# The probability blocks of neighbourhood attention go through DRAM, head by head, with the scores spaced evenly and six output tiles kept

## The chip, the cores and the metric

The kernel runs on one NeuronCore of one Trainium2 chip. The metric is device time in microseconds: 1574.57 us, the median of three runs before the change (1574.06 to 1577.02). The engines are named as in the profile: PE is TensorE (PEld its weight loads), DVE VectorE, ACT ScalarE, POOL GpSimd, SP the sync engine, which here only issues DMAs.

## The reference

The reference is one step of a trunk of two layers over 512 latent tokens (8 rows of 64) and 128 prompt tokens, 1024 wide. Layer 0 mixes by neighbourhood attention, layer 1 by grouped-query attention; a gated ConvFFN follows each. The change lies in layer 0's attention, of which this matters:

```
s_lat = einsum('brqhd,brkwhd->bhrqkw', qg, kg) * scale        # 8 x 16 window of keys, 16 heads of 64
s_lat = where(col_ok, s_lat + rpb[:, dr, dc], -inf)           # learned relative position bias
s_ctx = einsum('brqhd,bchd->bhrqc', qg, k_ctx) * scale        # 128 context keys
p     = softmax(concatenate([s_lat, s_ctx], -1), -1)
o     = einsum(p_lat, vg) + einsum(p_ctx, v_ctx)
op    = blocked_attention(qp, kp, vp)                         # the 128 prompt tokens
x     = x + gate * rmsnorm(o @ w_o)
```

## The kernel before, in words

All matrices are float32. A projection is split into a high and a low part of each operand (hi by a cast on ACT, lo by a subtraction on DVE or POOL), and three matmuls (hi·hi, hi·lo, lo·hi) stand for one. The weights come through four buffers `wr`, and their halves through four `wh` and four `wl`.

Layer 0's attention lasts from about 55 to 350 us. Three streams of work are interleaved in the order in which they are written, and each engine runs its part in order:

- `stream()` yields the projections in pieces. Each pair of heads has eight pieces of Q (`qk`, 256 columns for four, 384 for four) and eight of K; each group of four heads has fifteen pieces of V (`vp`). A piece is six to nine matmuls. `fill()` runs one piece. When the pieces are used up, the early part of the output projection (`y`, `m0.part0`) takes their place, three matmuls of 512 columns per piece.
- `ada0`, one step of which is eight small matmuls (`ada`) on two weight tiles of 512 KB, whose buffers are loaded again behind them.
- the heads. `Head.scores(slot)` handles one of four query blocks: two matmuls into `s` (L119), the bias and the running minimum on DVE (L980), the exponential on ACT (L984), the reciprocal on DVE (L988), the scaling on POOL (L989) and a transposition within 32 x 32 blocks on DVE (L992). The result stays in `p`.

A 32 x 32 transposition leaves each block in its own partitions. What is still wanted is an exchange of four partition groups of 32 with four blocks: block k of group q goes to block q of group k. The method `exchange` (L999) does this for a pair of heads by sixteen DMAs from `p` to `px`, both in SBUF, on SP's queue. `p` holds a pair and has two buffers, `px` holds a pair and has one.

`values` (L1004 on) multiplies V with `px` for a pair (24 matmuls into `po`) and ACT copies the result to the pair's output tile `of` (L1021). There are two such tiles; the first six pairs are written to DRAM (`of0d`, L486) and read back as `ofr` (L1032) when `o_split` makes the high and low part (`oh`, L1035, and `ol`, L1036) for the output projection. Every four heads the prompt's attention runs in three parts: `p0` scores (`sp`), `p1` transposes (`tp`), `p2` values (`po<-ptp`).

The order of the pieces in step h, in which head h + 1 is scored, is written in strings: `f` is a piece, `s0` to `s3` the scores, `x` the exchange, `v` the values, `a` a step of ada, `p0` to `p2` the prompt. `ORDER[0]` holds for even steps, `ORDER[1]` for odd ones, `ORDER0` for step 0 and `ORDER2` from step 13 on. A scheduler keeps PE in the written order and may move other engines' instructions a little past each other.

Of the kernel before, what the change touches and what calls it, by code (L numbers as in the profile page):

```python
# [40 lines left out]
NPX = 1  # L41
NOF = 2
# [9 lines left out]
ORDER0 = "s0 f s1 f f s2 f f s3 f f x f f a f f f f f".split()  # L52
ORDER = (
    "s0 f s1 f f s2 f f s3 f f x f f a f f f f f".split(),
    "p0 f f s0 f f p1 s1 f f s2 f f s3 f v a p2 f".split(),
)
ORDER2 = (
    ("s0 s1 f s2 f s3 f f x" + 16 * " f").split(),
    "p0 s0 f s1 f f p1 s2 f s3 f v p2 f".split(),
# [15 lines left out]
def raw_ap(ap, offset, dims):  # L75
    return bass.AP(tensor=ap.tensor, offset=ap.offset + offset, ap=[list(d) for d in dims])
# [30 lines left out]
def hybrid_step(ctx: ExitStack, tc: tile.TileContext, A, O):  # L107
# [19 lines left out]
    def f32(t):  # L127
        return t.bitcast(F32)
# [346 lines left out]
    of0, of0d = {}, {}  # L475
# [6 lines left out]

    def of_store(p):

        of0d[p] = dr.tile([P, T], F32, name=f"of0d{p}")
        nc.sync.dma_start(of0d[p], of0.pop(p))  # L486
# [300 lines left out]
    with l_na:  # L787
# [161 lines left out]
        pair, px = [None], [None]  # L949

        class Head:
# [42 lines left out]
            def exchange(self):  # L994

                px[:] = [ap.tile([P, 4, 2, 4, 3, QD], F32, tag="px", name="px", bufs=NPX)]
                for q in range(4):
                    for k in range(4):
                        nc.sync.dma_start(px[0][QD * k : QD * k + QD, q], self.pair[QD * q : QD * q + QD, k])  # L999

            def block(self, s0, s1):

                c0 = 12 * QD * self.b + 3 * QD * s0[0] + QD * s0[1]
                d = 3 * QD * (s1[0] - s0[0]) + QD * (s1[1] - s0[1])  # L1004
                return raw_ap(px[0], c0, [px[0].ap[0], [d, 2], [24 * QD, 4], [1, QD]])
# [22 lines left out]
        def o_split(p):  # L1028
            hi, lo = osp0[p]
            if p in of0d:  # L1030
                x = wp.tile([P, T], F32, tag="wr", name="ofr")
                nc.sync.dma_start(x, of0d[p])  # L1032
            else:
                x = of0[p]
            nc.scalar.copy(hi, x)  # L1035
            nc.vector.tensor_sub(lo, x, f32(hi))  # L1036
# [50 lines left out]
        for h in range(H):  # L1087
            nxt = Head(h + 1) if h + 1 < H else None
# [3 lines left out]
            for i, step in enumerate(order):  # L1092
                if step == "f":
                    if i < len(order) - 1 or h % 4 or not h:
                        fill()
                elif step == "a":
                    next(ada0, None)
                elif step[0] == "s" and nxt:
# [23 lines left out]
            if h % 2 and h < 12:  # L1122
                of_store(h // 2)
            before = head
# [859 lines left out]
```

## Time and profile before

| what | value |
|---|---|
| median of three runs | 1574.57 us |
| the profiled execution | 1577.02 us, its span 1575.0 us |
| granted clock of TensorE, mean of the span | 0.993 |
| PE, DVE, ACT, POOL busy, share of the span | 96%, 66%, 54%, 45% |
| HBM read and written | 216.34 and 28.31 MB, 155 GB/s over the span |
| exchanges of the sixteen heads | 128 DMAs of 96 KB |
| outputs stored and read back | 6 and 6 DMAs of 320 KB |

The profile page gives busy times and the groups of instructions; views of the trace give the waits of an engine by what released them, the instructions in order of time, and the busy time and granted clock of any stretch. A matmul's weights are loaded beside the previous matmul, so PE and PEld overlap. The duration of a matmul is modelled and overlaps the next; from start to start is the true spacing. A wait is put down to the semaphore that came last by the profile.

### The profile page before, as it was taken

Reading aid. Unit: us, or ns where it says so; the run is one execution under the profiler, and the core shown is the slowest. Engines: PE = TensorE matmul, PEld = TensorE weight load, DVE = VectorE, ACT = ScalarE, POOL = GpSimd, SP = SyncE. Lnnn points to the kernel's source line nnn. Section 1 sums busy time; section 2 is a strip of 40 time slices with the busy share of each in tenths; the row PEclk is TensorE's granted clock in tenths of the full one; section 3 lists DMA queues with packets and bytes.
Section 4 is the critical chain, followed back from the end, with each engine's and each line's share of the span. In section 5 each row is a group of like instructions: output and inputs, shape, how many; then the busy total and the mean of one; then the engine's idle time right before and its main releaser. Section 6 shows DMA issues by size and latency. Waiting matters only on the chain.

```text
span 1575.0 us, 25917 instructions
## 1 busy us (share of the span) xinstructions
PE 1507.6 (96%) x9549; PEld 1335.4 (85%) x9549; DVE 1037.2 (66%) x1680; ACT 843.3 (54%) x1608; POOL 710.2 (45%) x606
## 2 busy tenths in 40 slices
PE   6989999789999999999999999999999999999998
PEld 5978788568899999988887887877899999988886
DVE  4554444538887666776465878772988887886554
ACT  4554645535555555654544447773656665554443
POOL 1445535313445555534443555541325566553433
PEclk9999999999999999999999999999999999999999
DMA  9556767557366656368575331004633334448664
GB/s 325 140 154 178 203 154 213 150 163 249 105 206 198 218 194 194 104 222 289 178 244 184 101 108 55 2 1 166 203 110 114 106 110 151 132 155 267 215 220 136
DMA packets 204538, 260.50 MB, mean 165 GB/s; under 512 B 13724, under 2 KB 155260, under 8 KB 204412
## 3 DMA queue, kind: packets, MB, share of 16 engines
q1 hardware_dynamic: 194576, 252.27, 50.8%
q10 hardware_dynamic: 9836, 6.59, 2.2%
q8 instruction: 75, 1.23, 0.3%
q14 instruction: 51, 0.42, 0.1%
HBM read 216.34 MB, written 28.31 MB: 155 GB/s over the span
## 4 chain that ended last, share of the span: by engine, by line
PE 63%; DVE 5%; ACT 2%; issue 2%; POOL 1%; DMA 1%; ACTq 0%; POOLq 0%; DVEq 0%; SPq 0%
PE acc L119 18%; PE ux L119 17%; PE uz L119 8%; PE gp L119 5%; PE uy L119 4%; PE po L119 2%; PE y L119 2%; PE s L119 2%; PE tp L122 2%; PE ada L119 1%; DMA wr<-in_ffn_w_up 1%; DVE t L1303 1%; ACT gp L1714 1%; ACT t L1301 0%; DVE wl L182 0%
## 5 line engine op out<-in xcount | busy, mean ns | idle before, releaser
L182 POOL TENSOR_TENSOR wl<-wr,wh 128x1024 fp32r<-128x1024 f32 x70 | 172.8, 2474 | 240.8 <-ACT wh L180 231.1
L1226 POOL TENSOR_TENSOR wl<-wr,wh 128x1024 fp32r<-128x1024 f32 x76 | 183.6, 2439 | 42.2 <-ACT wh L1225 38.3
L119 PE MATMUL ux<-B,wh 128*128 128x322 f32 x832 | 201.0, 313 | 1.4 <-ACT u L1280 1.1
L1303 DVE SCALAR_TENSOR_TENSOR t<-C,cw,t 128x644 f32<-128x644 f32 x176 | 156.2, 888 | 55.5 <-ACT t L1301 54.9
L119 PE MATMUL acc<-wh,alo 128*128 128x512 f32 x440 | 172.3, 392 | 0.4 <-DVE alo L1195 0.3
L119 PE MATMUL acc<-wl,ahi 128*128 128x512 f32 x440 | 172.0, 391 | 0.0
L119 PE MATMUL acc<-wh,ahi 128*128 128x512 f32 x440 | 171.9, 391 | 0.0
L180 ACT CAST wh<-wr 128x1024 fp32r<-128x1024 f32 x140 | 145.6, 1049 | 43.3 <-DMA wr<-in_ffn_w_down 33.1
L119 PE MATMUL uz<-B,wh 128*128 128x322 f32 x640 | 156.2, 312 | 1.5 <-ACT v L1280 1.5
L119 PEld LDWEIGHTS ux<-B,wh 128*128 128x128 f32 x832 | 144.2, 189 | 4.4 <-ACT u L1280 2.2
L1195 DVE TENSOR_TENSOR alo<-ain,ahi 128x384 fp32r<-128x384 f32 (+1 forms) x88 | 82.7, 957 | 88.3 <-ACT ahi L1193 87.8
L119 PE MATMUL ux<-B,wl 128*128 128x322 f32 x416 | 129.9, 312 | 4.2 <-DVE wl L1226 4.2
L119 PE MATMUL qk<-hT,wh 128*128 128x384 f32 (+1 forms) x512 | 124.1, 315 | 1.7 <-DVE qs L892 1.7
L1226 POOL TENSOR_TENSOR vl<-wr,vh 128x1024 fp32r<-128x1024 f32 x38 | 106.2, 2794 | 26.2 <-ACT vh L1225 25.9
L119 PEld LDWEIGHTS uz<-B,wh 128*128 128x128 f32 x640 | 110.9, 189 | 4.9 <-ACT v L1280 2.0
L1225 ACT CAST wh<-wr 128x1024 fp32r<-128x1024 f32 x84 | 85.0, 1049 | 45.8 <-DVE wr L1249 45.3
L1301 ACT ACTIVATE t<-C,cw 128x644 f32<-128x644 f32 x88 | 78.6, 893 | 51.0 <-DVE C L1331 39.2
L182 DVE TENSOR_TENSOR wl<-wr,wh 128x1024 fp32r<-128x1024 f32 x70 | 91.7, 1320 | 17.3 <-ACT wh L180 16.7
L119 PE MATMUL uz<-B,wl 128*128 128x322 f32 x320 | 99.6, 311 | 0.4 <-POOL wl L1226 0.3
L119 PEld LDWEIGHTS acc<-wh,alo 128*128 128x128 f32 x440 | 82.6, 188 | 18.9 <-DVE alo L1195 1.2
L119 PEld LDWEIGHTS acc<-wl,ahi 128*128 128x128 f32 x440 | 82.6, 188 | 18.0 <-POOL wl L182 0.3
L119 PEld LDWEIGHTS acc<-wh,ahi 128*128 128x128 f32 x440 | 82.6, 188 | 17.8
(258 smaller groups left out, 3831.6 us busy)
## 6 DMA issues: line engine op xcount, KB each, us to landing
wr<-in_ffn_w_up SPq DMA_DIRECT2D x88, 512.0 KB
wr<-in_ffn_w_down SPq DMA_DIRECT2D x88, 512.0 KB
wr<-in_ada_w SPq DMA_DIRECT2D x72, 512.0 KB
act<-act SPq DMA_DIRECT2D x44, 321.0 KB
wr<-in_na_w_qkv SPq DMA_DIRECT2D x24, 512.0 KB
px<-p SPq DMA_DIRECT2D x128, 96.0 KB
mod<-modrow SPq DMA_DIRECT2D x20, 512.0 KB
ain<-act SPq DMA_DIRECT2D x44, 192.0 KB
```

The costliest lines, as they stand in the source:

```text
L119: pe(nc.tensor.matmul(*a, **k))
L122: pe(nc.tensor.transpose(*a, **k))
L180: i = nc.scalar.copy(hi, raw)
L182: j = (low or nc.vector).tensor_sub(lo, raw, f32(hi))
L1195: pin(nc.vector.tensor_sub(lo[:, 0 : c1 - c0], ain[:, 0 : c1 - c0], f32(hi[:, 0 : c1 - c0])))
L1225: nc.scalar.copy(hl[0], src)
L1226: low.tensor_sub(hl[1], src, f32(hl[0]))
L1301: nc.scalar.activation(t, taps(0), AF.Identity, bias=cw[:, 3, n : n + 1], scale=cw[:, 1, n : n + 1])
L1303: nc.vector.scalar_tensor_tensor(t, taps(d), cw[:, w, n : n + 1], t, op0=ALU.mult, op1=ALU.add)
L1714: nc.scalar.activation(self.pt[i].rearrange("p (a b) -> p a b", a=2), sv, AF.Exp, bias=nm, scale=-1.0, accum_out=su)
```

## The change

`exchange` is replaced by two methods. `write` stores a head's `p` to a DRAM tile `pd` in one DMA (128 rows of 6144 bytes, 768 KB). `read` loads it back into `px` in four DMAs, each of 32 partitions with four runs of 1536 bytes (192 KB). `p` now holds one head and still has two buffers; `px` holds a pair and has one. A head is written in the step that scores it (`w`; head 0 by `W` in step 0), read in the next step (`x`; the last head by `y`), and the values of a pair come in the even step after that. The four scores of a head are spread over a step, and the prompt's parts lie later in it. `of` has six buffers, and the store and reload of outputs are gone, so `o_split` reads `of` itself. The split of pair 6 follows the values in step 14, and the values of the last pair come after all early pieces of the output projection.

```diff
-NPX = 1
-NOF = 2
+NOF = 6
...
-    "s0 f s1 f f s2 f f s3 f f x f f a f f f f f".split(),
-    "p0 f f s0 f f p1 s1 f f s2 f f s3 f v a p2 f".split(),
+    "f s0 f s1 f v f s2 f x f a f f s3 f f f f w f".split(),
+    "s0 f f p0 f s1 f x f s2 p1 f a s3 f f p2 f f w".split(),
...
-    def of_store(p):
-
-        of0d[p] = dr.tile([P, T], F32, name=f"of0d{p}")
-        nc.sync.dma_start(of0d[p], of0.pop(p))
...
-                if not self.b:
-                    pair[:] = [ap.tile([P, 4, 2, 4, 3, QD], F32, tag="p", name="p", bufs=NPT)]
-                self.pair = pair[0]
-                self.p4 = self.pair[:, :, self.b]
+                self.p4 = ap.tile([P, 4, 4, 3, QD], F32, tag="p", name="p", bufs=NPT)
...
-            def exchange(self):
-
-                px[:] = [ap.tile([P, 4, 2, 4, 3, QD], F32, tag="px", name="px", bufs=NPX)]
-                for q in range(4):
-                    for k in range(4):
-                        nc.sync.dma_start(px[0][QD * k : QD * k + QD, q], self.pair[QD * q : QD * q + QD, k])
+            def write(self):
+
+                self.pd = dr.tile([P, 4, 12 * QD], F32, name=f"pd{self.h}")
+                nc.sync.dma_start(self.pd, self.p4.rearrange("p k n m i -> p k (n m i)"))
+
+            def read(self):
+
+                if not self.b:
+                    px[:] = [ap.tile([P, 4, 2, 12 * QD], F32, tag="px", name="px", bufs=1)]
+                self.px = px[0]
+                src = self.pd.rearrange("(q i) k c -> i q k c", q=4)
+                for k in range(4):
+                    nc.sync.dma_start(self.px[QD * k : QD * k + QD, :, self.b], src[:, :, k])
...
-            if p in of0d:
-                x = wp.tile([P, T], F32, tag="wr", name="ofr")
-                nc.sync.dma_start(x, of0d[p])
-            else:
-                x = of0[p]
-            nc.scalar.copy(hi, x)
-            nc.vector.tensor_sub(lo, x, f32(hi))
+            nc.scalar.copy(hi, of0[p])
+            nc.vector.tensor_sub(lo, of0[p], f32(hi))
...
-            nxt = Head(h + 1) if h + 1 < H else None
+            if h == H - 1:
+                break
+            nxt = Head(h + 1)
...
-                elif step == "x" and nxt:
-                    nxt.exchange()
-                elif step == "v":
-                    values((before, head))
+                elif step == "W":
+                    head.write()
+                elif step == "w":
+                    nxt.write()
+                elif step == "x":
+                    head.read()
+                elif step == "y":
+                    nxt.read()
+                elif step == "v" and h:
+                    values(done)
+                    if h == 14:
+                        o_split(6)
...
-            if h % 2 and h < 12:
-                of_store(h // 2)
-            before = head
+            if h % 2 == 0:
+                done = head, nxt
...
-            if h == 13:
-                o_split(6)
-            if h == 14:
-                drain(work)
-                for t in range(NT):
-                    m0.part0(t, 6)
+        drain(work)
+        for t in range(NT):
+            m0.part0(t, 6)
+        values(done)
         o_split(7)
```

SP's queue at the first heads, before. `px<-p` is an exchange, `wr<-in_na_w_qkv` a weight load of a projection (8x128 for Q or K, 4x256 for V), `wr<-in_ada_w` one of ada, `of0d` the store of an output:

```order
L176 DMA wr<-in_na_w_qkv 128x8x128
L999 DMA px<-p 32x768 x16
L295 DMA wr<-in_ada_w 128x1024 x2
L176 DMA wr<-in_na_w_qkv 128x4x256 x2
L295 DMA wr<-in_ada_w 128x1024 x2
L486 DMA of0d_1330<-of_1300 128x640
L176 DMA wr<-in_na_w_qkv 128x8x128 x4
L999 DMA px<-p 32x768 x16
L295 DMA wr<-in_ada_w 128x1024 x4
```

The same place with the change, from the V loads ahead of the first write to the loads behind head 2's write (`pd_970`, `pd_1114` and `pd_1311` are the DRAM tiles of heads 0 to 2):

```order
L175 DMA wr<-in_na_w_qkv 128x4x256 x2
L988 DMA pd_970<-p 128x1536
L997 DMA px<-pd_970 32x4x384
L294 DMA wr<-in_ada_w 128x1024 x2
L997 DMA px<-pd_970 32x4x384 x3
L988 DMA pd_1114<-p 128x1536
L175 DMA wr<-in_na_w_qkv 128x8x128
L294 DMA wr<-in_ada_w 128x1024
L997 DMA px<-pd_1114 32x4x384 x4
L294 DMA wr<-in_ada_w 128x1024
L988 DMA pd_1311<-p 128x1536
L175 DMA wr<-in_na_w_qkv 128x8x128 x2
```

The V weights of the second group stand before the first write instead of behind the first exchange. The Q load behind head 1's write is that of heads 6 and 7, the two behind head 2's write are K of these heads and Q of heads 8 and 9, which PE reaches in steps 3 and 4. Next in this queue come head 2's reads, two ada loads, head 3's write, two more ada loads and then head 3's reads.

PE at the start of step 1, before. `tk` transposes the new keys of the prompt for the output, `sp` is the prompt's scores, and `kh`, `kl` are the high and low part of the keys:

```order
L122 MATMUL tk<-ident,kp 128x128
L119 MATMUL sp<-kh_745,qs_673 128x128
L119 MATMUL sp<-kl_611,qs_673 128x128
L119 MATMUL sp<-kh_983,qs_829 128x128
L119 MATMUL sp<-kl_613,qs_829 128x128
L119 MATMUL sp<-kh_746,qs_674 128x128
L119 MATMUL sp<-kl_612,qs_674 128x128
```

The same place with the change:

```order
L121 MATMUL tk<-ident,kp 128x128
L118 MATMUL s<-kh_978,qs_829 128x384
L118 MATMUL s<-kl_613,qs_829 128x384
L118 MATMUL qk<-hT_114,wh 128x384
L118 MATMUL qk<-hT_114,wl 128x384
L118 MATMUL qk<-hT_115,wh 128x384
```

The first score of head 2, which needs the pair's new keys, now stands directly behind `tk`, and the prompt's scores follow after twelve matmuls of the projection.

SP's queue at the end of the stage, before:

```order
L1032 DMA ofr<-of0d_2926 128x640
L1032 DMA ofr<-of0d_3300 128x640
L176 DMA wr<-in_na_w_o 128x2x512 x4
L999 DMA px<-p 32x768 x16
L354 DMA mod<-modrow_2_83 128x1024
```

And with the change, from the write of head 14 on:

```order
L988 DMA pd_3591<-p 128x1536
L175 DMA wr<-in_na_w_o 128x2x512 x2
L997 DMA px<-pd_3591 32x4x384 x4
L988 DMA pd_3691<-p 128x1536
L175 DMA wr<-in_na_w_o 128x2x512 x2
L997 DMA px<-pd_3691 32x4x384 x4
L353 DMA mod<-modrow_2_83 128x1024
```

The last exchange has become head 15's write and its four reads, with two loads of output weights between them.

More of the change, by code (lines that the diff above doesn't have):

```diff
@@ L51 @@
 CTX = 2
-ORDER0 = "s0 f s1 f f s2 f f s3 f f x f f a f f f f f".split()
+ORDER0 = "s0 f f s1 f f W f f s2 f a f s3 f x f f f f f w".split()
 ORDER = (
-    "s0 f s1 f f s2 f f s3 f f x f f a f f f f f".split(),
-    "p0 f f s0 f f p1 s1 f f s2 f f s3 f v a p2 f".split(),
+    "f s0 f f s1 f v f s2 f x f a f f s3 f f f f w f".split(),
+    "s0 f f p0 f s1 f x f s2 p1 f a s3 f f p2 f f w".split(),
 )
 ORDER2 = (
-    ("s0 s1 f s2 f s3 f f x" + 16 * " f").split(),
-    "p0 s0 f s1 f f p1 s2 f s3 f v p2 f".split(),
+    "f s0 f s1 f v s2 f s3 f x f f f f f w f f f f f f y".split() + 12 * ["f"],
+    "s0 f x f s1 p0 f s2 f p1 s3 f p2 f f f f w".split(),
 )
@@ L474, in hybrid_step @@
     opool = r_na.enter_context(pool("o0", 1, "right"))
-    of0, of0d = {}, {}
+    of0 = {}
     def of_tile(p):
@@ L947, in na_table @@
             return tb
-        pair, px = [None], [None]
+        px = []
         class Head:
@@ L1004, in block @@
                 d = 3 * QD * (s1[0] - s0[0]) + QD * (s1[1] - s0[1])
-                return raw_ap(px[0], c0, [px[0].ap[0], [d, 2], [24 * QD, 4], [1, QD]])
+                return raw_ap(self.px, c0, [self.px.ap[0], [d, 2], [24 * QD, 4], [1, QD]])
         def values(two):
@@ L1097, in hybrid_step @@
                     next(ada0, None)
-                elif step[0] == "s" and nxt:
+                elif step[0] == "s":
                     nxt.scores(int(step[1]))
-                elif step == "x" and nxt:
-                    nxt.exchange()
-                elif step == "v":
-                    values((before, head))
+                elif step == "W":
[10 more added lines that the diff above has]
+                        o_split(6)
                 if pr and step == "p0":
```

## The prediction

> **What bounds the kernel now.** I read the page first, then who PE waits for in the stretch that the change touches, then the granted clock by ten microseconds, then the DMA queue of SP.
>
> ```profile
> span 1575.0 us, 25917 instructions
> PE 1507.6 (96%) x9549; PEld 1335.4 (85%) x9549; DVE 1037.2 (66%) x1680; ACT 843.3 (54%) x1608; POOL 710.2 (45%) x606
> DMA packets 204538, 260.50 MB, mean 165 GB/s; under 512 B 13724, under 2 KB 155260, under 8 KB 204412
> ```
>
> PE sets the end: it is busy for 96% of the span, and no other engine is above 66% (its weight loads overlap it). The change adds and removes no matmul, so it can move the time only through what PE loses between matmuls. It touches the neighbourhood attention, about 55 to 350 us. There PE waits for this (columns: who waits for whom, us in total, times, longest):
>
> ```profile
> PE vp L119 <- POOL wl L182: 6.9, 6, 2.5
> PE y L119 <- ACT oh L1035: 5.7, 2, 3.9
> PE po L119 <- DMA tr<-in_k_rpb: 3.7, 1, 3.7
> PE tk L122 <- ACT kp L906: 3.3, 1, 3.3
> PE vp L119 <- DVE kl L864: 3.2, 2, 1.6
> PE sp L119 <- ACT kh L863: 2.2, 5, 0.6
> PE tp L122 <- POOL pp L708: 1.8, 1, 1.8
> PE sp L119 <- DVE kl L864: 1.8, 7, 0.3
> PE qk L119 <- DVE qs L892: 1.7, 1, 1.7
> PE po L119 <- ACT qs L891: 1.6, 1, 1.6
> PE po L119 <- DMA px<-p: 1.2, 1, 1.2
> PE tk L122 <- DVE p L992: 1.0, 1, 1.0
> PE ada L119 <- DMA wr<-in_ada_w: 0.5, 1, 0.5
> ```
>
> These rows add up to 34.6 us. The second loss is the clock (columns by stretch: length, busy PE, PEld, DVE, ACT, POOL, granted clock, DMA share, GB/s):
>
> ```profile
> 90.00:100.00 10.00, 7.92 (x38) 7.36 (x39) 5.00 (x13) 6.00 (x20) 3.09 (x4) 0.83 0.56 122
> 110.00:120.00 10.00, 6.42 (x41) 5.78 (x38) 2.01 (x7) 5.30 (x14) 6.10 (x4) 0.94 0.94 273
> 120.00:130.00 10.00, 10.00 (x82) 9.28 (x82) 3.92 (x12) 5.52 (x12) 7.72 (x7) 0.89 0.80 177
> 240.00:250.00 10.00, 10.00 (x83) 7.89 (x82) 5.44 (x17) 6.43 (x20) 4.14 (x6) 1.00 1.00 298
> 280.00:290.00 10.00, 7.48 (x51) 5.12 (x52) 1.12 (x3) 1.14 (x4) 0.07 (x1) 0.83 0.64 183
> 310.00:320.00 10.00, 4.49 (x18) 2.93 (x20) 5.98 (x17) 4.52 (x13) 3.33 (x5) 0.84 0.67 192
> 320.00:330.00 10.00, 10.00 (x56) 7.34 (x53) 3.76 (x13) 4.25 (x13) 1.17 (x2) 0.82 0.44 156
> 90.00:350.00 260.00, 227.00 (x1587) 196.75 (x1588) 117.06 (x328) 129.59 (x357) 111.32 (x117) 0.97 0.67 181
> ```
>
> Each stretch below 1.00 follows waits, and loses ten times its missing share: 1.7 + 0.6 + 1.1 + 1.7 + 1.6 + 1.8 = 8.5 us. So 34.6 + 8.5 = 43.1 us is all that the change can work on. Most of it has nothing to do with the exchange itself; the queue that carries the exchange explains why:
>
> ```profile
> SPq L999 <- DVE p L992: 67.7, 8, 30.0
> 90.75 12.83 SPq L999 DMA_DIRECT2D px<-p  x16
> 104.79 0.94 SPq L176 DMA_DIRECT2D wr<-in_na_w_qkv  x2
> ```
>
> SP works in order. Its eight exchanges stand at the head of its queue for 67.7 us until the last probabilities are transposed, then hold it for about 12.8 us each, and what is traced behind them leaves late. The two V weight loads leave at 104.79, and their splits come too late for the V product: that is the wait of 2.5 us in the first row of PE's waits. The exchange costs PE more through what is queued behind it than through its own landing.
>
> **The change part by part.**
>
> *The SP queue.* In the new order the V weights stand ahead of the first write, and the Q and K loads follow writes whole heads before their use (the order of SP shows it). Behind a waiting write are then loads needed a head later, some 18 us (295 us for 16 heads), not the next ones. Of the 6.9 us for wl I leave 1.0, and with them goes the low clock of 110 to 130 us (0.6 + 1.1). Gain 5.9 + 1.7 = 7.6. SP itself issues 5 DMAs per head in place of 16 per pair, and no stores and reloads of outputs; it is off PE's path, so that is worth nothing by itself.
>
> *The exchange, longer and earlier.* It becomes a write of 768 KB and four reads of 192 KB per head. No row shows such a round trip. These are the nearest:
>
> ```profile
> px<-p SPq DMA_DIRECT2D x128, 96.0 KB
> of0d<-of SPq DMA_DIRECT2D x6, 320.0 KB
> 313.63 1.02 SPq L1032 DMA_DIRECT2D ofr<-of0d  x2
> 316.79 0.73 ACT L1035 CAST oh<-ofr 128x640 fp32r<-128x640 f32 x1 [1.20 <-DMA ofr<-of0d]
> 280.15 1.02 SPq L295 DMA_DIRECT2D wr<-in_ada_w  x2
> 281.99 4.50 PE L119 MATMUL po<-px,vt 128*64 128x256 f32 x24 [3.67 <-DMA tr<-in_k_rpb]
> ```
>
> A reload of 320 KB from DRAM is in use 3.2 us after its issue. The last part of an exchange, whose issue ended when the ada loads began at 280.15, was in use 1.8 us later (the row blames a table load, but it is the exchange that PE had been waiting for). With 1.8 us of latency and 298 GB/s, the rate of the stretch at full DMA share, 768 KB take 1.8 + 2.6 = 4.4 us, once written and once read.
>
> Cover in the new order: head 3's reads stand in SP behind the ada loads of its own step, which wait for PE's ada product. From there to the values PE has three scores, 24 matmuls of 384 columns and 24 of 256:
>
> ```profile
> 78.40 0.33 PE L119 MATMUL qk<-hT,wh 128*128 128x384 f32 x1
> 78.57 0.34 PE L119 MATMUL qk<-hT,wl 128*128 128x384 f32 x1
> 343.17 0.39 PE L119 MATMUL y<-wh,oh 128*128 128x512 f32 x1
> 343.40 0.39 PE L119 MATMUL y<-wl,oh 128*128 128x512 f32 x1
> 327.93 0.34 PE L119 MATMUL s<-kl,qs 128*128 128x384 f32 x1
> 331.11 1.14 DVE L992 STREAM_TRANSPOSE p<-p 128x384 f32<-128x384 f32 x2 [0.63 <-POOL p L989]
> ```
>
> One start follows the next after 0.17 us at 384 columns and 0.23 at 512, so about 0.12 at 256, by the columns. The cover is 6 x 0.17 + 24 x 0.17 + 24 x 0.12 = 8.0 us. The two ada loads of 512 KB and the reads make 1.8 MB, 6.2 + 1.8 = 8.0 us. It is even; I take 1.0 us of wait there and at heads 7 and 11, which have two loads ahead as well, and none at heads 1, 5, 9 and 13, which have at most one. The bounds are nothing, if a load is hidden, and 3.5 us each, if both come on top. For the last pair, head 15's scores to the values has 54 matmuls of 512 columns, 12.4 us. Against them: 4.3 us from the last score to its transpose (327.93 to 332.25), 4.4 to write, 4.4 to read: 13.1. Two output weight loads stand between write and reads, 3.5 us of traffic if none of it is hidden, so the wait lies between 0.7 and 4.2; I take 2.0. All: 3 x 1.0 + 2.0 = 5.0 us in place of 3.7 + 1.2 + 1.6 + 0.5 = 7.0; the clock term at 280 us I leave, for it can follow the last pair's wait. Gain 2.0.
>
> *The ring of six.* Twelve DMAs of 320 KB go. The output splits at the end of head 13's scores no longer wait for reloads: the 3.9 us of the longer oh wait becomes about 1.0, what one cast (0.73 us) and its subtraction take before the first product; the 1.9 us at the very end stays, since that chain is unchanged. One of the two clock stretches after 310 us goes, 1.7. Gain 2.9 + 1.7 = 4.6.
>
> *The scores, evenly spaced.* DVE, ACT and POOL do the same work in other places, so I price only the queueing: qs 1.7 to 0.5, kl before vp 3.2 to 1.6. The prompt scores move back by a score and two pieces of projection, but the first score of the next head now stands right behind tk and needs the same keys, so of tk, kh and kl (3.3 + 2.2 + 1.8 + 1.0 = 8.3) I keep 5.0. With half of the clock loss at 90 us that is 1.2 + 1.6 + 3.3 + 0.9 = 7.0. Against it, between the last prompt scores and their transposes PE now has six y matmuls and a score (1.7 us) where it had nine and two (2.8), so the 1.8 us for pp becomes 2.9: -1.1. Bounds: if the chains are as long as before, nothing is gained but the loss stays; if they never queue, all 13.2 + 1.7 go.
>
> *More traffic.* Writes and reads are 16 x 2 x 768 KB, against 128 x 96 KB and 12 x 320 KB: 8.7 MB more, 29 us at 298 GB/s. The stage has 260 x 0.67 = 174 us of DMA busy, so it goes to 203 of about 245, a share of 0.83. At least nothing, when all hides in idle queues; at most all 29 us. Since the loads stand a head ahead, I am near the lower end and take 4.
>
> Sum: 7.6 + 2.0 + 4.6 + 7.0 - 1.1 - 4.0 = 16.1 us. The profiled execution took 1577.02 us, with a span of 1575.0, so 1561 by its own time; it was the slowest of the three, and their median is 1574.57, which gives 1558.5. I forecast **1559 us**.
>
> On the clock, the rows show it lowered after gaps of 2.5 us in all (90 to 94 us). The Trainium skill ("TensorE: Matmul & The Clock Gate", What's actually happening) says that an idle window of about 3.4 us halves it and a busy one restores it. The 1.7 us lost per stretch agree with half rate for 3.4 us; the shortness of the gaps does not. By the rule only the waits of 3.7 and 3.9 us would be charged, the recovered clock would be 1.7 and not 4.3 us, and the time 1561.
>
> **The rivals.** *Only the reloads and the queue help* (the scores' chains stay as long): terms two and four vanish, the loss and the traffic stay: 7.6 + 4.6 - 1.1 - 4.0 = 7.1, **1567**. For it: p waits for POOL, whose order still mixes splits and products. Against it: each score then has a projection piece beside it.
>
> *The round trip through DRAM comes too late* (the slower side). Its place is the values; the price is the wait and 1.7 us of clock for each. If write and reads together land 5 us later than priced, heads 3, 7 and 11 wait 6.0 and the last pair 7.0: 25 + 4 x 1.7 = 31.8 in place of 5.0 + 1.7, 25 us more, and the gain turns into a loss: **1584**. It decides from about 16 us in all at these four places, 4 us each. For it: reads go in runs of 1536 bytes where the exchange had 3072, DMA share was already 0.94 and 1.00 in two stretches. Against it: three quarters of all packets are under 2 KB, and 298 GB/s were moved. The Trainium skill ("Perfetto Trace Analysis", DMA Optimizations) warns of overhead for DMAs under 2 KB and so speaks for this case; the packet row speaks against its weight here.
>
> *Nearly all waits go*: only 1.9 at the end, 2.0 for the last pair, its clock and 2 us elsewhere remain, 43.1 - 7.6 = 35.5, **1539**.
>
> *It does not do what it says*: SP's writes wait for the same p and its reads for the values before, so that loads leave as late as now; gains and the added traffic cancel, **1574**.
>
> **How the numbers follow.** Forecast 0.47, the smaller gain 0.20, nearly all 0.13, too late 0.14, no change 0.06. The range goes from 1545, between the forecast and the largest gain, to 1576, past the smaller gain and no change. What differs by less than 0.2% (3 us) can't be told from no change here. Faster: 0.47 + 0.13 + 0.18 of the smaller gain; same: 0.06 + 0.02; slower: 0.14.
>
> **What would show it.** Right: no PE wait for wl in vp above 1 us, SP's waits for p with no 30 us piece, no reload wait before oh, a PE time from first qk to last y shorter by about 16 us, waits of po for px of about 1 us at every second pair. Wrong: po waiting 4 us and more for px, the clock at 0.83 after each, a DMA share of 1.00 over whole heads, or ACT and DVE waits of PE as long as before under other names.

## The result, and the profile after

The changed kernel takes **1596.06 us** (median of four executions, 1589.01 to 1601.86) against 1574.85 us before (four, 1574.06 to 1577.02). The ratio is 1.013, 95% interval 1.0085 to 1.0176: slower by about 1.3%. The forecast was 1559 us, in a range of 1545 to 1576.

The page of the changed kernel begins so:

```profile
span 1587.1 us, 25863 instructions
PE 1514.9 (95%) x9549; PEld 1339.2 (84%) x9549; DVE 1036.0 (65%) x1680; ACT 842.5 (53%) x1608; POOL 699.9 (44%) x606
```

This execution took 1589.01 us, the fastest of its four; that of before, 1577.02, was the slowest of its own. The traces can account for the 12.0 us between these two, not for the whole 21.2 between the medians.

A common mark makes the stage comparable: the first matmul of the last part of the output projection starts at 348.92 us before and at 362.52 after. All loss lies ahead of it; behind it the changed kernel regains 1.5 us. Two rows give its parts, the stretch from 60 us to the mark (columns: length, busy PE, PEld, DVE, ACT, POOL, granted clock, DMA share, GB/s), of before

```profile
60.00:348.92 288.92, 254.00 (x1780) 222.94 (x1778) 134.84 (x383) 143.22 (x399) 127.06 (x133) 0.97 0.63 169
```

and of the changed kernel:

```profile
60.00:362.52 302.52, 261.63 (x1776) 227.26 (x1775) 136.24 (x384) 143.63 (x402) 127.25 (x133) 0.93 0.70 189
```

PE's idle time went from 34.9 to 40.9 us, 6.0 more. The same matmuls were busy for 261.6 in place of 254.0 us, 7.6 more, at a clock of 0.93 in place of 0.97. That is the whole 13.6. PE's waits after the change, 55 to 370 us:

```profile
PE po L118 <- DMA px<-pd: 18.3, 4, 6.3
PE qk L118 <- DVE qs L886: 9.8, 4, 3.2
PE tp L121 <- POOL pp L702: 6.2, 3, 5.3
PE s L118 <- DVE kl L858: 3.0, 1, 3.0
PE y L118 <- ACT oh L1028: 1.9, 1, 1.9
PE tk L121 <- ACT kp L900: 1.4, 1, 1.4
```

The many short waits of before have become few long ones. The waits for wl, for the reloaded outputs and for kl ahead of vp are gone; px, qs and tp have grown. Behind them stands a row that the prediction did not look at. POOL and DVE before, 60 to 370 us:

```profile
POOL tb L941 <- DMA tr<-in_k_rpb: 13.4, 3, 6.8
DVE p L992 <- POOL p L989: 53.4, 41, 5.4
```

And after the change:

```profile
POOL tb L935 <- DMA tr<-in_k_rpb: 45.4, 10, 6.4
DVE p L983 <- POOL p L980: 82.6, 51, 6.7
```

`tr` holds the raw bias runs of one head. POOL makes the bias table `tb` of a head from it in three operations, which stand among the scalings of an earlier head, and then three DMAs on ACT's queue fill the only `tr` buffer again. In both kernels the first operation of the next table stands behind the last scaling `p` of one head and ahead of the first scalings of the next, so the order on POOL is nearly the same. What has changed is the time between. POOL before, from head 3 to head 4 and from head 4 to head 5 (start, duration, in square brackets the idle time before and its releaser; the rows between are left out):

```profile
124.33 0.89 POOL L941 TENSOR_TENSOR tb<-mask,tr 128x256 f32<-128x256 f32 x1 [1.02 <-DVE nm L980]
134.93 2.41 POOL L182 TENSOR_TENSOR wl<-wr,wh 128x1024 fp32r<-128x1024 f32 x1 [4.44 <-issue]
137.28 0.89 POOL L941 TENSOR_TENSOR tb<-mask,tr 128x256 f32<-128x256 f32 x1
145.72 0.86 POOL L941 TENSOR_TENSOR tb<-mask,tr 128x256 f32<-128x256 f32 x1 [1.35 <-DVE nm L980]
152.77 0.88 POOL L941 TENSOR_TENSOR tb<-mask,tr 128x256 f32<-128x256 f32 x1 [5.54 <-DMA tr<-in_k_rpb]
154.06 0.59 POOL L989 TENSOR_SCALAR p<-p,rc 128x384 f32<-128x384 f32 x1 [0.41 <-DVE rc L988]
```

The last operation on the old runs starts at 124.33, the next table at 137.28, with the last scaling and weight splits between; by then the reload has landed, and nothing waits for it. At 152.77 POOL does wait for the reload, 5.54 us, but the scaling behind is not ready either: it waits another 0.41 us for its reciprocal `rc`. With the scores spread over the step, the first score of the next head follows the last of the old one sooner, and less time is left for the reload: the reciprocals of the last score of head 3 and of the first of head 4 start 12.9 us apart before (124.98 and 137.89) and 6.0 us apart after (129.19 and 135.23). Ten waits for `tr` are listed where there were three, and behind each the next operation starts at once. One of them is seen from 130 to 153 us of the changed kernel:

```profile
130.46 0.88 POOL L935 TENSOR_TENSOR tb<-mask,tr 128x256 f32<-128x256 f32 x1
131.37 1.90 ACTq L793 DMA_DIRECT2D tr<-in_k_rpb  x3
135.23 0.16 DVE L979 RECIPROCAL rc<-su 128x1 f32<-128x1 f32 x1 [1.84 <-ACT p L975]
138.25 0.86 POOL L935 TENSOR_TENSOR tb<-mask,tr 128x256 f32<-128x256 f32 x1 [6.35 <-DMA tr<-in_k_rpb]
139.06 2.40 POOL L181 TENSOR_TENSOR wl<-wr,wh 128x1024 fp32r<-128x1024 f32 x1
139.54 10.51 SPq L997 DMA_DIRECT2D px<-pd  x4
141.44 0.59 POOL L980 TENSOR_SCALAR p<-p,rc 128x384 f32<-128x384 f32 x1
142.06 0.58 DVE L983 STREAM_TRANSPOSE p<-p 128x384 f32<-128x384 f32 x1 [6.66 <-POOL p L980]
143.18 0.58 ACT L975 ACTIVATE p<-s,nm 128x384 f32<-128x384 f32 x1 [7.45 <-DVE nm L971]
146.74 0.39 DVE L320 TENSOR_TENSOR arow<-ada,abias 128x256 f32<-128x256 f32 x1
148.08 1.13 ACTq L327 DMA_DIRECT2D modrow<-arow  x2
152.76 3.68 PE L118 MATMUL po<-px,vt 128*64 128x256 f32 x16 [4.46 <-DMA px<-pd]
```

Read it downwards. The old runs are read at 130.46 and the reload is issued at 131.37. POOL stands for 6.35 us ahead of the next table, with a weight split and a scaling behind it whose reciprocal was there at 135.4; the scaling starts at 141.44. DVE, in order, stands for 6.66 at the transposition of the scaling that POOL delays; ACT for 7.45 at the exponential behind it. The `arow` addition and ACT's store `modrow` are in those queues and leave at 146.74 and 148.08. The last of the four reads of head 3, whose data have nothing to do with `modrow`, waits 5.5 us for that store, and PE waits 4.46 us for the read. Why a read should wait for a foreign store is told by the instruction list of the changed kernel, where brackets name the semaphores (the first and the last of the four reads):

```
L997 DMA px<-pd_1520 32x4x384 [waits DMAHW0_49]
L997 DMA px<-pd_1520 32x4x384 [waits DMAHW4_49]
```

The first waits for the write ahead of it. The last, like the two between, waits for nothing but a completion semaphore, and the user of this one ahead of it is the first `modrow` store. There are eight of these in the list, DMAHW0 to DMAHW7, used in turn by the DMAs of SP and ACT together; as list and trace read together, a DMA waits until the earlier user of its semaphore has landed.

### The profile page after: what moved, and what is told of

Same layout as the page of the kernel before. It is cut to its first block, busy times and chain, and to the rows that moved or that the text cites. A ratio compares the mean times of both kernels' runs of the same rounds, so it can differ in the third digit from the quotient of the medians.

```text
span 1587.1 us, 25863 instructions
## 1 busy us (share of the span) xinstructions
PE 1514.9 (95%) x9549; PEld 1339.2 (84%) x9549; DVE 1036.0 (65%) x1680; ACT 842.5 (53%) x1608; POOL 699.9 (44%) x606
## 4 chain that ended last, share of the span: by engine, by line
PE 63%; DVE 6%; issue 3%; DMA 3%; ACT 3%; POOL 2%; ACTq 0%; SPq 0%; POOLq 0%; DVEq 0%
PE ux L118 18%; PE acc L118 15%; PE uz L118 8%; PE y L118 5%; PE uy L118 5%; PE gp L118 3%; PE po L118 3%; PE s L118 2%; PE tp L121 2%; PE ada L118 1%; DMA wr<-in_ffn_w_down 1%; POOL wl L181 1%; DVE wl L181 1%; DVE t L1303 1%; DMA wr<-in_ffn_w_up 1%
## 5 line engine op out<-in xcount | busy, mean ns | idle before, releaser
L118 PE MATMUL qk<-hT,wh 128*128 128x384 f32 (+1 forms) x512 | 127.8, 323 | 9.8 <-DVE qs L886 9.8
L1226 POOL TENSOR_TENSOR vl<-wr,vh 128x1024 fp32r<-128x1024 f32 x38 | 96.3, 2533 | 24.6 <-ACT vh L1225 24.3
L1301 ACT ACTIVATE t<-C,cw 128x644 f32<-128x644 f32 x88 | 78.6, 893 | 50.9 <-DVE C L1331 38.8
L118 PEld LDWEIGHTS qk<-hT,wh 128*128 128x128 f32 x512 | 92.8, 197 | 14.4 <-DVE qs L886 7.7
L118 PEld LDWEIGHTS acc<-wl,ahi 128*128 128x128 f32 x440 | 82.6, 188 | 18.8 <-POOL wl L181 0.9
```

What stands on the lines that cost most here:

```text
L118: pe(nc.tensor.matmul(*a, **k))
L1226: low.tensor_sub(hl[1], src, f32(hl[0]))
L1301: nc.scalar.activation(t, taps(0), AF.Identity, bias=cw[:, 3, n : n + 1], scale=cw[:, 1, n : n + 1])
```

## Experiments

Times stand against the kernel before in the same session, whose median there was 1574.4 to 1576.5 us. The first four runs were to tell POOL's wait for `tr` from the DRAM path and from the spacing of the scores.

**A second buffer for tr.**

```diff
-                tr = tpool.tile([P, 2, RUN], F32, tag="tr", name="tr", bufs=1)
+                tr = tpool.tile([P, 2, RUN], F32, tag="tr", name="tr", bufs=2)
```

> The changed kernel with a second buffer for the bias runs (tr), nothing else. Theory POOL (the table of the next head stands in POOL's order ahead of the last scalings of this head and waits there for the reload of the only tr buffer; the scalings, the transpositions on DVE, Q's low part and the write to DRAM are all late behind it): POOL's wait for tr falls from 45.4 us to under 10, PE's wait of qk for qs from 9.8 to under 3, the po wait for px from 18.3 to under 9, and the time from 1596 to about 1575. Theory DRAM (the round trip is too long and the added traffic slows all transfers): the wait for tr may fall, but po still waits 15 us or more for px and the time stays above 1588.

1576.18 us, ratio 1.0002 (0.9987 to 1.0018): this one number takes back the whole loss. PE's waits, 55 to 370 us:

```profile
PE po L118 <- DMA px<-pd: 11.5, 3, 4.6
PE tp L121 <- POOL pp L702: 6.4, 4, 4.6
PE qk L118 <- DVE qs L886: 5.4, 4, 2.3
PE tk L121 <- ACT kp L900: 4.2, 1, 4.2
```

POOL's wait for `tr` falls from 45.4 to 6.1 us and DVE's for POOL's `p` from 82.6 to 50.9; the mark is back at 348.92. The waits for px and qs fell less than forecast, to 11.5 and 5.4 us (below 9 and 3 were expected). The wait for px falls by 6.8 us although nothing on the exchange's path was touched.

**The exchange in SBUF**, head by head in sixteen DMAs at the place of the reads, the rest as changed.

```diff
-                self.pd = dr.tile([P, 4, 12 * QD], F32, name=f"pd{self.h}")
-                nc.sync.dma_start(self.pd, self.p4.rearrange("p k n m i -> p k (n m i)"))
+                return
...
+                for q in range(4):
+                    for k in range(4):
+                        nc.sync.dma_start(self.px[QD * k : QD * k + QD, q, self.b], src[QD * q : QD * q + QD, k])
```

> The changed kernel with its spacing and its ring of six, but each head's blocks go from p to px directly, by sixteen DMAs of 48 KB at the place of the reads, and nothing is written to DRAM. Theory DRAM: the waits of po for px fall under 5 us in all and the time falls to 1575 or below. Theory POOL: POOL's wait for tr stays above 30 us and PE's wait for qs above 6; the time stays between 1582 and 1592.

1594.02 us, ratio 1.0105 (1.0075 to 1.0135). Without the round trip through DRAM the loss remains, and POOL still waits 34.5 us for `tr`; the time is 2 us above the range of the POOL theory. The DRAM path is not the main cause.

**The DRAM path alone, in the kernel before**: one write of 1536 KB and four reads of 384 KB per pair, in the place of the sixteen exchanges.

```diff
-                for q in range(4):
-                    for k in range(4):
-                        nc.sync.dma_start(px[0][QD * k : QD * k + QD, q], self.pair[QD * q : QD * q + QD, k])
+                nc.sync.dma_start(pd, self.pair.rearrange("p k b n m i -> p k (b n m i)"))
...
+                for k in range(4):
+                    nc.sync.dma_start(dst[QD * k : QD * k + QD], src[:, :, k])
```

> The kernel before with only the path of the exchange changed: at the place of the sixteen DMAs one write of the pair (1536 KB) to DRAM and four reads of 384 KB. Theory DRAM: po waits for px more than in the kernel before by 2 us and more per pair, and the time is 10 us or more above 1575. Theory POOL: POOL's order is as before, its wait for tr stays at about 13 us, and the time is within 5 us of 1575, since the sixteen DMAs held SP for 10 to 13 us as well.

1604.84 us, ratio 1.0174 (1.0143 to 1.0205). I had put it within 5 us; the forecast of the DRAM theory came true here. PE and SP, 55 to 372 us:

```profile
PE po L119 <- DMA px<-pd: 40.7, 8, 6.8
SPq L1002 <- DMA pd<-p: 36.7, 8, 5.6
```

The first read of each pair waits 4.6 us on average for the write ahead of it. The round trip is longer than the old place covers, by about 5 us per pair (its write is twice as large as one of the change). So with a DRAM path the later place of the reads in the change is needed; the same path with the reads of one head at the old place was not run.

**The spacing alone, in the kernel before**, with its exchange per pair and two output tiles. (It is close to that of the change, not the same: there the even order begins `f s0 f f s1`, with two pieces ahead of `s1`, where the diff of the change above prints one, and the orders of step 0 and from 13 on differ too.)

```diff
-    "s0 f s1 f f s2 f f s3 f f x f f a f f f f f".split(),
-    "p0 f f s0 f f p1 s1 f f s2 f f s3 f v a p2 f".split(),
+    "f s0 f s1 f f s2 f f a f f s3 f f f x f f f".split(),
+    "s0 f f p0 f s1 f f s2 p1 f a s3 f f p2 f v f".split(),
```

> The kernel before with only the scores spread over the step and the prompt's parts later, as in the change; exchange in SBUF per pair, two output tiles. Theory POOL: POOL's wait for tr rises from 13.4 to 25 us or more, the new waits of qk for qs appear, and the time is 3 to 12 us above 1575. Theory DRAM: the spacing helps as forecast, waits for wl, kh, kl and qs fall, and the time is 3 to 10 us below 1575.

1600.69 us, ratio 1.0145 (1.0113 to 1.0176). POOL's wait for `tr` doubles, from 13.4 to 27.4 us:

```profile
POOL tb L941 <- DMA tr<-in_k_rpb: 27.4, 6, 8.1
PE po L119 <- DMA tr<-in_k_rpb: 24.0, 2, 12.2
```

So the spacing of the scores brings more of POOL's wait. The loss of 24 us is twice what the theory had at most (3 to 12). The spacing also moves the exchange closer to the values, which I could not keep apart here: I put the waits of po (24.0, and 10.0 more that the trace puts down to issue) down to that, which no run shows.

**Two more with one condition less.** The SBUF form with two `tr` buffers (the first two diffs together) asks what the DRAM path is worth once POOL does not wait:

> The changed kernel with two tr buffers and the exchange inside SBUF again, sixteen transfers per head at the place of the reads, no DRAM. If the whole loss was GpSimd's order (theory), it is within 4 us of the kernel with two buffers and the DRAM path (1576.2), so 1572 to 1580, with POOL's wait on tr below 10 us. If the round trip through DRAM costs time of its own at this spacing (rival), it is at least 6 us faster than that: below 1570. If sixteen transfers on SyncE's queue are what costs (second rival), it stays above 1585 as the one-buffer form did (1594.0).

1584.08 us, ratio 1.0058 (1.0041 to 1.0074), between what I had given for the theory (to 1580) and for the second rival (above 1585). The second buffer gains 10 us here too (POOL's wait for `tr` is 13.4 us in place of 34.5; below 10 was expected), but 8 us remain against the DRAM form. Of PE's waits two rows show where:

```profile
PE ada L118 <- DMA wr<-in_ada_w: 10.5, 6, 3.1
PE po L118 <- DMA px<-p: 7.4, 1, 7.4
```

PE waits for weight loads that stand behind the sixteen DMAs, and for the exchange of one pair. At this spacing, write and four reads through DRAM are the better exchange, in spite of the added traffic.

**Table behind the last scaling**, one `tr` buffer: only the order on POOL is changed. All three operations of a head's table now stand behind the last scaling of the head just before it. (The expectation says "as in the kernel before"; that is not so. In that kernel, as in the changed one, they stand among the scalings of the head two places earlier.)

```diff
-                if h == 2:
+                if h >= 2:
                     behind(i, plast[0])
...
-                if not self.h:
-                    plast[:] = [i]
+                plast[:] = [i]
```

> The changed kernel, its single bias buffer tr kept; only the place of the first table operation of each next head in GpSimd's order changes: behind the last scaling p of the head before it, as in the kernel before. If the loss is GpSimd standing still for the reload of tr in front of scalings that are ready (theory), VectorE's wait on POOL p falls from 82.6 us to 50-58, GpSimd's wait on tr from 45 us to below 20, SyncE's writes are no longer late, TensorE's wait on px falls from 18.3 to 8-13, and the time is 1573 to 1582 (ratio 0.999 to 1.005), about what the second buffer gave (1576.2). If the second buffer helped because the transfers themselves start earlier (rival), the reload ends as late as now, the waits on tr stay above 35 us, and the time stays at 1588 to 1600. If the table then comes too late for the first scores of the next head (second rival), VectorE's row of s waits on POOL tb by 15 us or more and the time is 1583 to 1590.

1588.77 us, ratio 1.008 (1.0056 to 1.0104). My theory fell as I had put it, and so did the second rival: DVE's score additions wait 1.0 us for `tb`, not 15. No table of POOL waits for `tr` any more, and DVE's wait for `p` is down from 82.6 to 45.5 us, but PE's waits for px and qs are still there:

```profile
PE po L118 <- DMA px<-pd: 16.7, 4, 6.2
PE qk L118 <- DVE qs L886: 12.6, 4, 5.8
```

Some 7 us came back at most: the medians differ by 7.3 us, but the two profiled executions by 0.2 (1589.01 and 1588.81), and the intervals of the two ratios overlap. Where the others are is shown by ACT in this kernel, 162 to 169 us:

```profile
166.21 0.57 ACTq L793 DMA_DIRECT2D tr<-in_k_rpb  x1
166.87 0.27 ACT L911 COPY ko<-tk 128x128 f32<-128x128 f32 x1 [4.05 <-POOL tb L935]
168.95 0.38 ACT L885 ACTIVATE qs<-qk 64x256 fp32r<-64x256 f32 x1
```

The reload's issue stands on ACT until POOL has read the old runs, with `ko`, an exponential and the `qs` copy behind it; PE then waits 5.79 us for `qs`. SP's waits that end on `tr`, 60 to 350 us, add up to 83.6 us here, 57.5 in the changed kernel and 33.5 before. The handshake over one buffer has two ends, and I had moved one.

**The reload on POOL's own queue**, one `tr` buffer, the table where the change puts it: the other end.

```diff
-        def na_runs(h, q=nc.scalar):
+        def na_runs(h, q=nc.gpsimd):
```

> The changed kernel with its one tr buffer; only the reloads of tr are issued on GpSimd's own queue, where the table operation that frees the buffer stands directly ahead, instead of on ScalarE's. The table moved behind the last scaling took GpSimd's wait away and yet gained only some 7 us, so a second half of the handshake is suspected: the reload waits on ScalarE for the buffer to come free, with ScalarE's copies behind it, and SyncE's reads and weight loads wait for the reload (57.5 us of SyncE's waits end on tr in the changed kernel, 33.5 before), as they share eight completion semaphores in turn with it. If this half counts (theory), no wait of ScalarE or SyncE ends on tr, TensorE's wait on px falls from 18.3 us to below 12 and on qs from 9.8 to below 6, and the time is 1575 to 1585. If only GpSimd's own wait for the landing counts (rival), that wait stays at 35 us or more and the time at 1586 to 1600; issuing three transfers per head on GpSimd may cost it as much again: then above 1600.

1595.86 us, ratio 1.0132 (1.0097 to 1.0167), the rival's time. Yet two of the theory's rows came as written: no wait of ACT or SP ends on `tr`, and PE's wait for px falls from 18.3 to 5.3 us. (That for qs is 7.0, where below 6 was expected.) The line does two things that no run keeps apart: it takes the reload off ACT's queue, and off the eight semaphores that SP and ACT share. POOL's end is still there, and PE now waits elsewhere (9.5 us for the copy `kp` on ACT, 5.9 for kl). DVE still waits 83.5 us for POOL's `p`, and POOL for `tr`:

```profile
POOL tb L935 <- DMA tr<-in_k_rpb: 34.4, 11, 7.2
```

**Both ends at once**, the two diffs above together, still one buffer.

> The changed kernel with its one tr buffer and both halves at once: the first table operation of each next head stands behind the last scaling of the head before, and the reloads of tr are issued on GpSimd's own queue. Moved table alone gave 1588.8, moved reload alone 1595.9. If the loss is the handshake over one buffer, whose two ends stood in queues ahead of other work (theory), neither end now stands ahead of anything ready: GpSimd's wait on tr stays below 15 us, no wait of ScalarE or SyncE ends on tr, and the time is 1573 to 1580, as with two buffers. If a table that begins only behind the last scaling is itself too late for the next head's scores (rival), VectorE's score additions wait on POOL tb, the waits on qs and px stay above 25 us in sum, and the time is 1584 to 1592.

1574.33 us, ratio 0.9998 (0.9984 to 1.0012). Each end alone gave 7 us at most and nothing; both give 22, as much as the second buffer. Neither POOL nor ACT nor SP shows a wait that ends on `tr`, and of the wait for px almost nothing is left:

```profile
PE qk L118 <- DVE qs L886: 12.2, 4, 4.9
PE po L118 <- DMA px<-pd: 3.4, 3, 2.8
```

This settles the cause of the loss: the only `tr` buffer, whose release and reload stood in two in-order queues ahead of work that was ready. Not every wait goes with it: that for qs is 12.2 us here, longer than in the changed kernel, and 5.4 with two buffers.

**The same line in the kernel before**, as a control: `q=nc.gpsimd` in place of `q=nc.scalar`, nothing else.

> The kernel before, with one line changed: the reloads of tr on GpSimd's queue. It tells how much of the best version (1565.3 us, 9.8 below before) the old order would have had from that line. If SyncE's waits on tr (33.5 us) and ScalarE's (6.7) delayed nothing that TensorE waits for (theory, as TensorE's idle time there is 34.9 us with no long wait behind a tr reload but one of 3.7), the time is 1572 to 1577. If they held the weight loads (rival), the waits on wl of 6.9 us go and the time is 1565 to 1570. If GpSimd then waits for tr ahead of its scalings as in the changed kernel with one buffer (second rival), it is above 1582.

1580.86 us, ratio 1.0035 (1.0021 to 1.0049): slower by 5 us, which none of the three had. DVE's wait for POOL's `p` rises from 53.4 to 65.4 us; 39 issues take POOL's time, 23 us in all. The old order has nothing to gain from that line.

**Reads earlier, and the prompt spread**, with two `tr` buffers.

```diff
-    "s0 f f p0 f s1 f x f s2 p1 f a s3 f f p2 f f w".split(),
+    "s0 p0 f f x f s1 f f s2 f p1 f a s3 f p2 f f w".split(),
```

> The changed kernel with two tr buffers, and the odd heads' order written so that the four reads come three fills earlier, ahead of the weight loads of the adaptive norm on SyncE's queue (they stood behind two such loads there), and that five fills rather than three lie between the prompt scores and their turn. If the waits on px (11.5 us in three) and tp (6.4 us in four) come from those places (theory), both fall below 3 us in sum, 10 to 14 us of TensorE's idle time go, and the time is 1561 to 1569. If the work that fills is merely used up earlier (rival), other waits (qs, kl, kh, the first y) grow by as much and the time is 1573 to 1579.

(The expectation miscounts: the reads are two fills earlier, not three, and six fills, not five, lie between `p0` and `p1`.) 1572.66 us, ratio 0.9979 (0.9966 to 0.9992). The gain of 3.5 us over two buffers alone lies below the rival's range by a hair and above the theory's. The wait for px hardly moved, from 11.5 to 10.6, and tp fell from 6.4 to 4.6, so neither wait went as expected.

**The same with the reload on POOL's queue** (`q=nc.gpsimd` again)**:**

> The kernel with two tr buffers and earlier reads (1572.7 us), with the reloads of tr issued on GpSimd's queue. If the waits of ScalarE and SyncE that end on tr (12.9 and 38.1 us there) still delay the reads (theory), TensorE's wait on px falls from 10.6 to below 6 us and the time is 1563 to 1569. If they delay nothing that TensorE waits for (rival), 1571 to 1575. If GpSimd's time to issue delays the scalings p (second rival), VectorE's wait on POOL p rises from 49.5 us to above 65 and the time is 1577 or more.

**1565.31 us, ratio 0.9935 (0.9914 to 0.9956)**, the best of all and faster than both kernels. The time is in the theory's range, its row is not:

```profile
PE po L118 <- DMA px<-pd: 11.5, 4, 5.0
```

The wait for px stays at 11.5 us. The profiled executions of this kernel and the one above differ by 1.9 us only (1567.92 and 1569.78), and the mark lies at 341.64 and 340.25, so the traces do not show where the median's 7 us come from; the two were timed in different sessions. That stays open. Against the kernel before, the mark is 7.3 us earlier, of 9.1 us between the two profiled executions and 9.8 between the medians.

**The same order with one buffer and both ends moved:**

> The changed kernel with its one tr buffer, the table behind the last scaling and the reload on GpSimd's queue (1574.3 us), and with the odd heads' order of the earlier experiment: the four reads two fills earlier, six fills rather than three between the prompt scores and their turn. If the order is worth as much here as it was with two buffers (3.5 us, 1576.2 to 1572.7) and the waits on qs and tk stay (theory), the time is 1568 to 1573. If the second buffer is needed for the best time (rival), it stays at 1573 to 1577; if the order with the freed queues is worth what both gave together with two buffers (second rival), it reaches 1563 to 1567.

1571.62 us, ratio 0.9977 (0.9964 to 0.999), in the theory's range and 2.7 below the same kernel with the changed order. The wait for px is back at 11.2, so the order's gain is again not in that row. (The profiled execution, 1577.93 us, was the slowest of its ten.)

The ring of six output tiles could not be tried alone: with `p` for a pair, as before, SBUF has no room for six. The kernel before has no room for a second `tr` buffer either.

## Why the prediction was wrong, step by step

- **The SP queue** (gain 7.6): right. No wait for wl is left in PE's waits after the change, and the granted clock is 1.00 from 110 to 140 us. (The exchanges of before held SP for 10.0 to 13.8 us, not 12.8 each; no term rests on that.)
- **The exchange** (four waits, 1.0, 1.0, 1.0 and 2.0): the places were right, at heads 3, 7, 11 and the last pair, the sizes not: 4.46, 6.29, 5.32 and 2.25 us, 18.3 for 5.0. The rival "too late" gave 16 us as the point from which the gain turns into a loss, and 1584 us; 18.3 us and a loss are its side. But its reason, a slow round trip, is not what sets the kernels apart. With both ends of the handshake moved, the same round trip leaves 3.4 us, and SP's reads wait as long for their writes there (24.6 us) as in the changed kernel (24.9). What differs is how long these reads stand behind foreign DMAs: 52.3 us in the changed kernel, 40.9 with two buffers, 17.2 with the reload on POOL's queue, 11.7 with both ends moved. PE's wait for px goes the same way: 18.3, 11.5, 5.3, 3.4 us. The kernel with two buffers, the other odd order and the reload on POOL breaks the row, with 9.1 and 11.5, so this is not all of it. The rival's runs of 1536 bytes decide nothing here: the DMAs carry 192 and 768 KB, and the exchange in SBUF head by head has the same runs.
- **The ring** (gain 4.6): the 3.9 us wait for the reloaded output is gone, the 1.9 at the end stays, as forecast. The clock stretch after 310 us did not go; the longer wait for tp (5.29 us at 328.71) stands there now.
- **The scores, evenly spaced** (gain 7.0, loss 1.1): **this is the step that failed.** It said that "DVE, ACT and POOL do the same work in other places, so I price only the queueing". The same operations at other times did cost: the time between two heads that had covered the reload of the only `tr` buffer was gone, and POOL's wait for it grew by 32 us, to 45.4. With this wait taken away, by a second buffer or by both ends moved, 20 and 22 us come back, where 21 were lost. In the changed kernel qs went from 1.7 to 9.8 where 0.5 was forecast, and tp from 1.8 to 6.2 where 2.9 was. Only tk, kh and kl, at 4.4 with the wait of the scores, are near the forecast 5.0. The row of POOL's wait on `tr`, 13.4 us before, was there to be read; I had looked at SP's and PE's order only.
- **More traffic** (4.0): not measured by itself. With two `tr` buffers the stage moves 197 GB/s in place of 169 and the time is that of before; the SBUF form with less traffic is 8 us slower. Nothing here speaks for a price of its own.
- **The clock**, which I had counted as a follower of the waits, made more than half of the loss: 7.6 of 13.6 us.

The handshake explains why the kernel is slower than before, not why the forecast 16.1 us are missing: with it removed, the design as it stands is worth nothing measurable (ratios 1.0002 and 0.9998). The stretch up to the mark shows where they went in the kernel with two buffers (columns as in the first such row):

```profile
60.00:348.92 288.92, 257.95 (x1789) 223.91 (x1788) 136.40 (x384) 143.23 (x400) 128.91 (x134) 0.96 0.73 197
```

PE idles 31.0 us there, 3.9 less than before, where the terms had 15.8 less; and it is busy for 258.0 us in place of 254.0, at a clock of 0.96 in place of 0.97, where the terms had 4.3 less. So some waits went, and others took their place: px 11.5 us where 5.0 was forecast, tp 6.4 where 2.9, qs 5.4 where 0.5. The sizes of the exchange and of the scores' chains would have been wrong without the handshake too; what sets them stays open. With another order of the odd steps and the reload on POOL, the design is worth 0.65%.

## What to carry to other kernels

When a change moves work in time and leaves its amount on an engine alone, look all the same for an operation of that engine that waits for a single buffer's reload, and ask what time covers this reload before and after: when the cover goes, the operations behind it inherit the wait, on that engine and on the queue that issues the reload. A handshake over one buffer has two such ends, and moving either alone may show nothing; a second buffer, or release and reload on one queue behind what is ready, takes both away. A DMA may also be late because of a DMA that it shares nothing with but a completion semaphore, so look at what the trace names as the releaser before blaming the transfer.

## What the runs showed of the hardware

The clock is not lowered by the length of a gap alone. In the kernel with two `tr` buffers and the changed order, PE waited 2.33 us at 87 us (columns of the second fence as in the table of stretches above):

```profile
87.33 0.36 PE L118 MATMUL qk<-hT,wh 128*128 128x256 f32 x1 [2.33 <-DVE qs L886]
```

```profile
85.00:90.00 5.00, 2.67 (x22) 2.71 (x23) 2.76 (x9) 2.98 (x10) 2.62 (x4) 1.00 0.90 274
90.00:95.00 5.00, 3.33 (x18) 2.56 (x17) 2.38 (x6) 3.64 (x8) 2.27 (x3) 1.00 0.41 104
```

With the reads earlier, the same wait of 2.32 us came 0.25 us later:

```profile
87.58 0.36 PE L118 MATMUL qk<-hT,wh 128*128 128x256 f32 x1 [2.32 <-DVE qs L886]
```

```profile
85.00:90.00 5.00, 2.68 (x16) 2.45 (x15) 2.96 (x10) 3.23 (x11) 2.61 (x4) 0.83 0.89 229
90.00:95.00 5.00, 4.51 (x27) 4.06 (x26) 2.38 (x6) 3.39 (x8) 2.29 (x4) 0.83 0.42 105
```

One lost no clock, the other 2 x 5 x 0.17 = 1.7 us. The Trainium skill ("TensorE: Matmul & The Clock Gate", What's actually happening) has the clock halved after an idle window of about 3.4 us. Half rate for 3.4 us is 1.7, so the size agrees; the gap that lowered the clock here, 2.32 us, is shorter than that. Why one of the two gaps did and the other did not was not tried.

The other surprise is how long DMAs stand behind foreign ones by the completion semaphores. SP's reads of `px` waited 52.3 us on foreign DMAs in the changed kernel (sum of its waits on `tr`, `modrow`, the caches, weights and outputs, 60 to 350 us); the sixteen exchanges per pair of the kernel before, 4.8. What this cost PE by itself was not measured.
